# Half of the conditioning's steps in the top-16 search instead of the delta rule, and the low parts of 68 down tiles on VectorE instead of GpSimd

## The chip, the core and the metric

One core of one Trainium2 chip runs one program: two transformer blocks on 512 tokens of width 1024, in fp32. The metric is the device time of one execution in microseconds; the kernel before takes 2505.04 us, the median of three runs (2502.44 to 2505.36). Engines are called as in the profile: PE (TensorE, matmuls), DVE (VectorE), ACT (ScalarE), POOL (GpSimd), SP (SyncE, whose queue issues most DMAs).

## What is computed

The first block is a mixer (a gated delta rule on one half of the width, a pooled branch on the other), and PEER, a layer of 16,384 experts of which each token uses 16 per head. The second block is modulated by a conditioning vector. Cut to what the change touches:

```python
def second_block(x, c, ada_w, ada_b, ...):
    mod_all = einsum('bd,lde->lbe', silu(c), ada_w) + ada_b      # 1 x 6*1024: six rows
    ...
def _peer(xn, w_query, sub_keys, expert_down, expert_up):        # per block of 128 tokens
    q = (xb @ w_query).reshape(t, 8, 2, 128)
    scores = einsum("thpc,hpkc->thpk", q, sub_keys)
    s1, i1 = top_k(scores[:, :, 0], 16); s2, i2 = top_k(scores[:, :, 1], 16)
    cand = s1[..., :, None] + s2[..., None, :]                   # 16 x 16 candidates a head
    top_s, top_pos = top_k(cand, 16)
    gate = softmax(top_s)
    act = gelu(einsum("td,thkd->thk", xb, expert_down[idx]))
    return einsum("thk,thkd->td", gate * act, expert_up[idx])
```

The six rows of `mod_all` depend on `c` and `ada_w` alone. They are read by the second block, which is behind PEER.

## The kernel before

**Precision.** A product of fp32 matrices is made from three matmuls (`mm3`): each operand is split in a high part, a cast to fp32r, and a low part, the rest. `split` loads a weight tile of 128 x 1024 into a buffer with the tag `raw`, casts it on ACT (L186) and subtracts on DVE or on POOL (L187), whichever its caller hands over as `lo_engine`. `wform` makes a split and eight times three matmuls with it (L197 high by high, L198 low by high, L199 high by low). The ring of `raw` buffers has four places, and splits, the conditioning and the norms share it. High and low parts have rings of their own (`wh`, `wl`: two each).

**The stages**, in the profiled execution's time: norm, projections and the pooled branch (0 to 170 us); the delta rule (170 to 370); what is left of the conditioning, and w_out (370 to 431); the norm before PEER (431 to 463); the search for the 16 best keys and candidates (`topk`, 463 to 582); decoding of the positions into key numbers (the last part of `topk`, 582 to 672); the gates, one-hot rows of keys multiplied to a dense table (`gates`, 672 to 991); eight down tiles (to 1037); the up products (to 1790); and the second block.

**The conditioning** is the generator `ada`. It makes the six rows one after another, a segment of ten steps each: eight steps load a tile of 512 KB (SP), scale it by silu(c) on ACT (L1142) and, from the second on, add it to `ada_acc` on POOL (L1144); one step splits the sum in high (ACT, L1150) and low (POOL, L1151), sums over partitions with a matrix of ones on PE (L1155, L1156) and adds to the row on DVE (L1157); the last multiplies on POOL and reduces on DVE, or multiplies and stores. The row, the high and the low part, and one more buffer in two segments, are `raw` buffers too. In the kernel before, each round of the delta rule's loop `together` takes one step, and what is left after the loop runs at its end:

```python
                next(self.side, None)
...
        for rest in (filler, self.side):
            for _ in rest:
                pass
```

`filler` is there `pool_out`, the products of the mixer's output with w_out and their addition to x.

**The down tiles.** Of 128 tiles of `expert_down` 74 (`SPILL`) are made before the up products and stored to memory; the generator `spill` yields after each. `fill(n)` takes n of them: 0, 1, 0, 1, 0, 1, 0 and 3 after the heads of the search (`FILL_QUERY`, 6 in all), 3 before each of four token tiles of decoding (12), one after every second bank of the gates (48), and what is left, 8, afterwards. The other 54 are made among the up products. For 128 of the tokens the experts' rows are gathered one by one from POOL's queue (`sparse`, L920) and multiplied on DVE (L933); so the dense tiles have 384 columns.

**The search** runs over 16 c's (a head and a half of its query): a query (`wform` on w_query, POOL low part, read by ACT at L989) one ahead, its products with the keys, and four top-16 searches on DVE. After two c's come the head's 50 candidates (L1011) and their search.

**The gates** make, for eight tokens at a time, one-hot rows A (L1106) and E (L1107) and three products B = E x gate part (L1109) on DVE, 24 matmuls (L1114), and take one step of `sparse`.

**The order** on each engine is set by a scheduler that simulates the program with its own estimate of each instruction when the kernel is built; the order in which the code issues is its input. At run time each engine goes through its list in order.

Of the kernel before, what the change touches and what calls it, by code (L numbers as in the profile page):

```python
# [5 lines left out]
F32R = mybir.dt.float32r  # L6
# [8 lines left out]
P = 128  # L15
ST = 512
NT = 4
D = 1024
# [8 lines left out]
FILL_QUERY = [0, 1, 0, 1, 0, 1, 0, 3]  # L27
# [15 lines left out]
    [(1, 4), (1, 5)], [(1, 6)],  # L43
]
ATT_ABS = [(0,), (1,)]
FILL_DECODE = 3
FILL_GATES = 2
REST = 208
# [86 lines left out]
class Net:  # L135
# [238 lines left out]
    def mixer1(self, qk):  # L374
        nc, d = self.nc, self.d
# [23 lines left out]
        with self.sb("ap1") as self.ap:  # L399
            hT = self.norm_begin()  # L400
            with self.sb("px") as self.np:
                self.np_tag, self.np_bufs = "xhat", 6
                rest = [self.norm_tile(hT, 0, small[:, 0:8])]
# [170 lines left out]
        self.tap("gc", gc)  # L574
        self.ahead = [self.split(d["w_out"][4 + k], "u", nc.gpsimd) for k in range(4)]
        with self.sb("gd") as gd:
            self.side = self.ada(gd)
            self.delta(gd, qT, kT, vb, zs, oh, ol, beta, g, gc, egc, begc, egl, masks, self.pool_out(ph, pl, oh, ol))
        return oh, ol

# [51 lines left out]
    def delta(self, gd, qT, kT, vb, zs, oh, ol, beta, g, gc, egc, begc, egl, masks, filler):  # L632
        nc, d = self.nc, self.d
# [146 lines left out]
        def together(*gens):  # L780
            live, n = list(gens), 0
            while live:
                n += 1
                if n in FILL_DELTA:
                    next(filler, None)
                next(self.side, None)
                for gen in list(live):
                    if next(gen, self) is self:
                        live.remove(gen)
# [12 lines left out]
                yield from finish(T)  # L802

        together(scans(), lane(0), lane(1), lane(2))
        for rest in (filler, self.side):
            for _ in rest:
                pass

# [1 line left out]
    def peer(self, xT, stop=None):  # L812
        nc, d = self.nc, self.d
        nb = DT // 32
        G_d = self.t(self.dp, [nb, P, P, 32], tag="gates")
        act_d = self.t(self.dp, [SPILL, P, DT], tag="acts")
        with self.sb("pact") as pact:
# [7 lines left out]
            def spill():  # L825
                for n, j in enumerate(range(SPILL)):
                    stored[j] = n
                    nc.sync.dma_start(act_d[n], self.down(pact, j, xT, nc.gpsimd))
                    yield

            filler = spill()
# [8 lines left out]
            with self.sb("pm") as pm:  # L840
                self.sparse_pool = pm, ("su",), 6
                acc = {(T, dh): self.bank() for T in range(1, NT) for dh in range(2)}
# [9 lines left out]
                for n in range(len(tiles) + LOOK):  # L852
                    if n < len(tiles):
                        j = tiles[n]
# [116 lines left out]
    def topk(self, pi, xT, stop):  # L971
        nc, d = self.nc, self.d
# [4 lines left out]
        with self.sb("pk") as pk:  # L977
# [3 lines left out]
            I = self.t(pk, [P, NT, 16, 16], U32, tag="I")  # L981
            TV = self.t(pk, [P, NT, 8, 16], tag="TV")
            TI = self.t(pk, [P, NT, 8, 16], U32, tag="TI")
            queries = {}

            def query(c):
                pm = self.wform(d["w_query"][c], xT, nc.gpsimd)
# [4 lines left out]
            for h in range(8):  # L992
                for p in range(2):
                    c = 2 * h + p
                    if c < 15:
                        query(c + 1)
                    q = queries.pop(c)
                    pss = self.bank()
                    for T in range(NT):
                        nc.tensor.matmul(pss[:, T * P:(T + 1) * P], q[:, T * P:(T + 1) * P], sk[:, c, :],  # L1000
                                         start=True, stop=True)
                    S = self.t(pk, [P, NT, P], tag="S", bufs=2)
                    nc.scalar.activation(S, pss.rearrange("p (a b) -> p a b", a=NT), AF.Copy)
                    for T in range(NT):
                        self.top16(pk, V[:, T, c, :], I[:, T, c, :], S[:, T, :], P)

                C = self.t(pk, [P, NT, 50], tag="C", bufs=2)
                off = 0
# [114 lines left out]
                nc.sync.dma_start(G_d[tb], stg)  # L1123


    def ada(self, pool):

# [1 line left out]
        nc, d = self.nc, self.d  # L1131
        cp, sc = self.mp, self.silu_c
        raw_tile = lambda dt=F32: self.t(self.wp, [P, D], dt, tag="raw", bufs=self.raw_bufs)
        self.mod = {}
        ones = self.t(pool, [P, P], F32R, tag="ones_r")
        nc.gpsimd.tensor_copy(ones, self.ones)
        for seg, name in enumerate(("sh_m", "sc_m", "gt_m", "sh_f", "sc_f", "gt_f")):
            acc = self.t(pool, [P, D], tag="ada_acc", bufs=1)
            for k in range(KT):
                raw = raw_tile()  # L1140
                nc.sync.dma_start(raw, d["ada_w"][seg, k])
# [7 lines left out]
            hi, lo = raw_tile(F32R), raw_tile(F32R)  # L1149
# [9 lines left out]
            if gate:  # L1159
                g = raw_tile()  # L1160
                n = 1 if name == "gt_m" else 2
# [297 lines left out]
```

## Time and profile before

| | us |
|---|---|
| median of three runs | 2505.04 |
| lowest and highest run | 2502.44, 2505.36 |
| profiled execution, its own time | 2507.3 |
| its span | 2505.5 |
| busy: PE, DVE, POOL, ACT | 2286.2, 1729.1, 1056.4, 944.4 |
| mean granted clock of PE | 0.962 |

A row of a timeline gives the start, the length, the engine, the line and operation, what is written <- what is read, and in brackets how long the engine stood idle ahead of it and what ended that. Neighbouring instructions of one kind are one row with their count, and the length is then that of the run. A row of a group gives the count, the busy time, the mean of one in ns, and the idle time before the group with what ended most of it; a row by tile or line gives lowest, middle and highest duration in ns. The page's slices show PE at nine tenths or more from 1000 us on, and below before that; that earlier part is where the change lies.

### The profile page before, as it was taken

The page shows a single profiled execution, that of the slowest core. Times are in us where ns is not written, and L with a number is a line of the kernel's source. Part 1 is how long each engine was busy: PE and PEld are TensorE (multiplying, and loading weights), DVE is VectorE, ACT ScalarE, POOL GpSimd, SP SyncE. Part 2 cuts the span into 40 slices and gives each one's busy share as a digit, 9 for nine tenths or more (in the row PEclk, how much of TensorE's full clock was granted, in tenths as well). Part 3 has the DMA queues.
Part 4 walks back from the last instruction along what each step waited for, and adds up shares of the span by engine and source line. Part 5 has one row for each costly group of instructions (what it writes and reads, how often), then busy time and mean ns, then how long its engine had stood idle before and what let it go on. Part 6 is the DMA issues. An engine that isn't in the chain of part 4 may idle for free.

```text
span 2505.5 us, 31798 instructions
## 1 busy us (share of the span) xinstructions
PE 2286.2 (91%) x11953; PEld 1924.0 (77%) x11953; DVE 1729.1 (69%) x2741; ACT 944.4 (38%) x1416; POOL 1056.4 (42%) x613
## 2 busy tenths in 40 slices
PE   7978972996788889999999999999899999999998
PEld 6758751885788888888888888888777666888887
DVE  6685532799699997488787888888855664433334
ACT  4254233333333333333333333333436665422222
POOL 4356356246655555465555565665312331000000
PEclk9989985998899999999999999999999999999999
DMA  4223244322577777789899999998531121422231
GB/s 159 68 84 119 68 152 150 121 94 87 198 253 273 267 250 264 256 303 330 309 327 312 338 325 333 317 333 304 173 118 42 43 68 59 135 95 93 91 100 60
DMA packets 179851, 467.91 MB, mean 187 GB/s; under 512 B 15344, under 2 KB 83952, under 8 KB 178032
## 3 DMA queue, kind: packets, MB, share of 16 engines
q1 hardware_dynamic: 141824, 329.33, 38.8%
q0 software_dynamic: 36864, 134.23, 15.0%
q10 hardware_dynamic: 1008, 2.31, 0.3%
q8 instruction: 93, 1.52, 0.2%
q14 instruction: 62, 0.51, 0.1%
HBM read 420.86 MB, written 44.96 MB: 186 GB/s over the span
## 4 chain that ended last, share of the span: by engine, by line
PE 48%; DVE 3%; DMA 3%; issue 2%; POOL 1%; ACT 1%; SPq 0%; DVEq 0%; POOLq 0%; ACTq 0%
PE bank L198 15%; PE bank L197 15%; PE bank L199 15%; PE bank L1336 4%; DMA raw<-in_e_down_dram 1%; DMA act<-acts 1%; DVE ul L187 1%; POOL wl L187 1%; DVE su L933 0%; DVE x L939 0%; DMA raw<-in_f_out_dram 0%; ACT uh L186 0%; POOL su L920 0%; DVE act L866 0%; DMA raw<-in_e_up_dram 0%
## 5 line engine op out<-in xcount | busy, mean ns | idle before, releaser
L199 PE MATMUL bank<-actT_h,wl 128*128 128x384 f32 (+2 forms) x1672 | 596.9, 357 | 70.4 <-POOL wl L187 70.4
L197 PE MATMUL bank<-actT_h,wh 128*128 128x384 f32 (+2 forms) x1672 | 599.8, 359 | 15.2 <-ACT actT_h L328 11.6
L198 PE MATMUL bank<-actT_l,wh 128*128 128x384 f32 (+2 forms) x1672 | 591.1, 354 | 1.2 <-DVE actT_l L330 1.2
L187 POOL TENSOR_TENSOR wl<-raw,wh 128x1024 fp32r<-128x1024 f32 x157 | 416.4, 2654 | 269.6 <-ACT wh L186 175.8
L186 ACT ACTIVATE wh<-raw 128x1024 fp32r<-128x1024 f32 x190 | 201.1, 1058 | 588.4 <-issue 366.8
L199 PEld LDWEIGHTS bank<-actT_h,wl 128*128 128x128 f32 x1672 | 319.6, 191 | 107.3 <-POOL wl L187 85.6
L197 PEld LDWEIGHTS bank<-actT_h,wh 128*128 128x128 f32 x1672 | 320.3, 192 | 41.5 <-ACT actT_h L328 12.8
L198 PEld LDWEIGHTS bank<-actT_l,wh 128*128 128x128 f32 x1672 | 320.2, 192 | 24.5 <-DVE actT_l L330 1.4
L186 ACT ACTIVATE uh<-raw 128x1024 fp32r<-128x1024 f32 x194 | 202.9, 1053 | 279.6 <-PE bank L199 143.7
L187 DVE TENSOR_TENSOR ul<-raw,uh 128x1024 fp32r<-128x1024 f32 x167 | 227.1, 1363 | 117.3 <-ACT uh L186 116.7
L197 PE MATMUL bank<-uh,ah 128*128 128x512 f32 x768 | 303.8, 396 | 0.3 <-ACT ah L867 0.3
L199 PE MATMUL bank<-uh,al 128*128 128x512 f32 x768 | 302.5, 396 | 1.6 <-DVE al L868 1.6
L198 PE MATMUL bank<-ul,ah 128*128 128x512 f32 x768 | 303.8, 396 | 0.0
L920 POOL DMA_INDIRECT su<-in_e_up_dram,rows_of x128 | 195.1, 1524 | 173.2 <-DVE x L939 150.3
L259 POOL TENSOR_TENSOR rs<-ms,nhalf 128x1 f32<-128x1 f32 (+1 forms) x23 | 15.6, 679 | 446.0 <-DVE ms L258 446.0
L1109 DVE TENSOR_TENSOR B<-E,g 128x1024 bf16<-128x1024 bf16 x144 | 190.3, 1372 | 0.0
L939 DVE SCALAR_TENSOR_TENSOR x<-su,own_act,x 128x1024 f32<-128x1024 f32 x128 | 178.7, 1396 | 1.1
L199 PEld LDWEIGHTS bank<-uh,al 128*128 128x128 f32 x768 | 144.3, 188 | 37.2 <-DVE al L868 2.5
L197 PEld LDWEIGHTS bank<-uh,ah 128*128 128x128 f32 x768 | 144.3, 188 | 33.6 <-ACT ah L867 1.4
L198 PEld LDWEIGHTS bank<-ul,ah 128*128 128x128 f32 x768 | 144.3, 188 | 32.6
L920 POOL DMA_INDIRECT su<-in_e_rows_dram,rows_of x76 | 106.3, 1399 | 96.7 <-DVE su L933 81.8
L866 DVE TENSOR_TENSOR act<-act,G 128x384 f32<-128x384 f32 x128 | 91.7, 730 | 76.2 <-DMA act<-acts 45.3
(392 smaller groups left out, 3833.6 us busy)
## 6 DMA issues: line engine op xcount, KB each, us to landing
raw<-in_e_down_dram SPq DMA_DIRECT2D x128, 512.0 KB
raw<-in_e_up_dram SPq DMA_DIRECT2D x128, 512.0 KB
raw<-in_ada_w_dram SPq DMA_DIRECT2D x48, 512.0 KB
gates<-stg SPq DMA_DIRECT2D x12, 2048.0 KB
G<-gates SPq DMA_DIRECT2D x32, 768.0 KB
raw<-in_f_in_dram SPq DMA_DIRECT2D x44, 512.0 KB
acts<-act SPq DMA_DIRECT2D x74, 192.0 KB
act<-acts SPq DMA_DIRECT2D x74, 192.0 KB
```

Source lines behind the costliest of these rows:

```text
L186: nc.scalar.activation(hi, raw, AF.Copy)
L187: (lo_engine or nc.vector).tensor_sub(lo, raw, hi.bitcast(F32))
L197: nc.tensor.matmul(ps, l[0], r[0], start=start, stop=False)
L198: nc.tensor.matmul(ps, l[0], r[1], start=False, stop=False)
L199: nc.tensor.matmul(ps, l[1], r[0], start=False, stop=stop)
L259: nc.gpsimd.tensor_tensor(r, ms, self.nhalf.to_broadcast([P, n]), op=OP.pow)
L866: nc.vector.tensor_tensor(av, av, G[:, :, j % 4, :], op=OP.mult)
L920: nc.gpsimd.indirect_dma_start(out=t, out_offset=None, in_=down if n < P else up, in_offset=bass.IndirectOffsetOnAxis(ap=self.rows_of[:, n ...
L939: nc.vector.scalar_tensor_tensor(x0, t, act[:, c:c + 1], x0, op0=OP.mult, op1=OP.add)
L1109: made = nc.vector.tensor_tensor(B[:, k], E, bc(parts[k]), op=OP.mult)
L1336: self.nc.tensor.matmul(o, l, r, start=start, stop=stop, skip_group_check=True)
```

## The change

Two things. First, `ada` takes a step only in the first 30 rounds of the delta rule (`ADA_DELTA`), which are the first three of its six segments. The other 30 steps are taken in the search, two after each c; 15 of the 16 c's suffice. `ada_acc` is allocated in the search's pool there, and the matrix of ones in a pool that lives longer. Second, the low part of a down tile made ahead is subtracted on DVE if it is the seventh or a later one: 68 tiles, which are the 12 in decoding, the 48 in the gates and the 8 behind them. Those in the search and those among the up products stay on POOL.

```diff
+ADA_DELTA = 30
 ...
         with self.sb("gd") as gd:
-            self.side = self.ada(gd)
+            ada, self.ada_pool = self.ada(), gd
+            self.ada_steps = lambda n: [next(ada, None) for _ in range(n)]
 ...
                 if n in FILL_DELTA:
                     next(filler, None)
-                next(self.side, None)
+                if n <= ADA_DELTA:
+                    self.ada_steps(1)
 ...
         together(scans(), lane(0), lane(1), lane(2))
-        for rest in (filler, self.side):
-            for _ in rest:
-                pass
+        for _ in filler:
+            pass
 ...
                 for n, j in enumerate(range(SPILL)):
                     stored[j] = n
-                    nc.sync.dma_start(act_d[n], self.down(pact, j, xT, nc.gpsimd))
+                    lo = nc.gpsimd if n < sum(FILL_QUERY) else nc.vector
+                    nc.sync.dma_start(act_d[n], self.down(pact, j, xT, lo))
                     yield
 ...
-            queries = {}
+            queries, self.ada_pool = {}, pk
 ...
                     for T in range(NT):
                         self.top16(pk, V[:, T, c, :], I[:, T, c, :], S[:, T, :], P)
+                    self.ada_steps(2)
 ...
-    def ada(self, pool):
+    def ada(self):
 ...
-        ones = self.t(pool, [P, P], F32R, tag="ones_r")
+        ones = self.t(cp, [P, P], F32R, tag="ones_r")
 ...
-            acc = self.t(pool, [P, D], tag="ada_acc", bufs=1)
+            acc = self.t(self.ada_pool, [P, D], tag="ada_acc", bufs=1)
```

The lines behind the changed ones have numbers up to four higher in the changed kernel: L187 becomes L188, L933 L936, L1106 L1110, L1107 L1111, L1109 L1113, L1144 L1148, L1155 L1159.

**PE at the end of the delta rule**, before: `raw` is the high or low part of a conditioning segment, `uh` and `ul` w_out's parts, `oh` and `ol` the mixer's output; bank_2553 is the second half of token tile 1, bank_2708 tile 2.

```order
L199 MATMUL bank_2553<-uh_2403,ol_97 128x512
L1156 MATMUL bank_2538<-raw_2535,ones_r_1299 128x512
L1156 MATMUL bank_2542<-raw_2535,ones_r_1299 128x512
L1155 MATMUL bank_2608<-raw_2604,ones_r_1299 128x512
L1155 MATMUL bank_2612<-raw_2604,ones_r_1299 128x512
L1156 MATMUL bank_2608<-raw_2605,ones_r_1299 128x512
L1156 MATMUL bank_2612<-raw_2605,ones_r_1299 128x512
L1155 MATMUL bank_2658<-raw_2654,ones_r_1299 128x512
L1155 MATMUL bank_2662<-raw_2654,ones_r_1299 128x512
L197 MATMUL bank_2708<-uh_2385,oh_96 128x512
```

The same place of the change (bank_2507 is tile 1's second half, bank_2558 tile 2):

```order
L200 MATMUL bank_2507<-uh_2389,ol_97 128x512
L198 MATMUL bank_2507<-uh_2395,oh_96 128x512
L199 MATMUL bank_2507<-ul_2396,oh_96 128x512
L200 MATMUL bank_2507<-uh_2395,ol_97 128x512
L198 MATMUL bank_2558<-uh_2377,oh_96 128x512
L199 MATMUL bank_2558<-ul_2378,oh_96 128x512
L200 MATMUL bank_2558<-uh_2377,ol_97 128x512
```

The matmuls of three segments that stood between the products of tile 1 and those of tile 2 have left this place.

**POOL in the search**, before, where the low parts of queries and down tiles follow one another:

```order
L187 TENSOR_TENSOR wl_3027<-raw_3024,wh_3026 128x1024
L187 TENSOR_TENSOR wl_3125<-raw_3122,wh_3124 128x1024
L187 TENSOR_TENSOR wl_3189<-raw_3186,wh_3188 128x1024
L187 TENSOR_TENSOR wl_3287<-raw_3284,wh_3286 128x1024
L187 TENSOR_TENSOR wl_3321<-raw_3318,wh_3320 128x1024
```

The change there, around the end of a segment (L1155 is the low part of the conditioning's sum, L1173 the multiplication of its row):

```order
L1148 TENSOR_TENSOR ada_acc_2874<-ada_acc_2874,raw_3124 128x1024
L188 TENSOR_TENSOR wl_3169<-raw_3166,wh_3168 128x1024
L1148 TENSOR_TENSOR ada_acc_2874<-ada_acc_2874,raw_3128 128x1024
L188 TENSOR_TENSOR wl_3203<-raw_3200,wh_3202 128x1024
L1155 TENSOR_TENSOR raw_3267<-ada_acc_2874,raw_3266 128x1024
L188 TENSOR_TENSOR wl_3284<-raw_3281,wh_3283 128x1024
L1173 TENSOR_TENSOR raw_3264<-raw_3264,consts_68 128x1024
L1148 TENSOR_TENSOR ada_acc_3345<-ada_acc_3345,raw_3349 128x1024
L188 TENSOR_TENSOR wl_3390<-raw_3387,wh_3389 128x1024
```

Between two low parts of weights there now stand one or two instructions of the conditioning.

**DVE in the gates**, before, a little over one period (`uh` and `ul` at L933 are gathered rows):

```order
L933 SCALAR_TENSOR_TENSOR uh_5092,own_act_2925<-uh_5092,xs_2912 128x1024
L1109 TENSOR_TENSOR B_5390<-E_5389,g_981_5004 128x1024
L1109 TENSOR_TENSOR B_5390<-E_5389,g_982_5005 128x1024
L1109 TENSOR_TENSOR B_5390<-E_5389,g_983_5006 128x1024
L933 SCALAR_TENSOR_TENSOR ul_5165,own_act_2925<-ul_5165,xs_2912 128x1024
L1107 TENSOR_TENSOR E_5462<-keys_4998,i2b_5001 128x1024
L1106 TENSOR_TENSOR A_5461<-keys_4998,i1b_5000 128x1024
```

The same place of the change:

```order
L936 SCALAR_TENSOR_TENSOR ul_5165,own_act_2775<-ul_5165,xs_2762 128x1024
L188 TENSOR_TENSOR wl_5353<-raw_5350,wh_5352 128x1024
L1110 TENSOR_TENSOR A_5461<-keys_4998,i1b_5000 128x1024
L1111 TENSOR_TENSOR E_5462<-keys_4998,i2b_5001 128x1024
L1111 TENSOR_TENSOR E_5535<-keys_4998,i2b_5001 128x1024
L188 TENSOR_TENSOR wl_5426<-raw_5423,wh_5425 128x1024
L1110 TENSOR_TENSOR A_5534<-keys_4998,i1b_5000 128x1024
L1110 TENSOR_TENSOR A_5609<-keys_4998,i1b_5000 128x1024
L1113 TENSOR_TENSOR B_5463<-E_5462,g_981_5004 128x1024
L1113 TENSOR_TENSOR B_5463<-E_5462,g_982_5005 128x1024
L1113 TENSOR_TENSOR B_5463<-E_5462,g_983_5006 128x1024
L936 SCALAR_TENSOR_TENSOR uh_5238,own_act_2775<-uh_5238,xs_2762 128x1024
```

Two low parts of down tiles stand in DVE's list for every two periods, beside the one-hot rows of both, and the products B follow them.

## The prediction

> **What bounds the kernel now.** I read the engines' line and the chain that ended last first, then busy times cut into the stretches that the change touches: what the conditioning leaves after the delta rule, the search (its last 14 us apart), decoding, gates, and the eight down tiles behind the gates.
>
> ```profile
> PE 2286.2 (91%) x11953; PEld 1924.0 (77%) x11953; DVE 1729.1 (69%) x2741; ACT 944.4 (38%) x1416; POOL 1056.4 (42%) x613
> PE 48%; DVE 3%; DMA 3%; issue 2%; POOL 1%; ACT 1%; SPq 0%; DVEq 0%; POOLq 0%; ACTq 0%
> core 0: us, PE busy (x) PEld busy (x) DVE busy (x) ACT busy (x) POOL busy (x), PEclk, DMA share, GB/s
> 358.00:431.00 73.00, 18.63 (x57) 13.02 (x55) 18.41 (x18) 24.69 (x24) 52.44 (x23) 0.62 0.47 154
> 462.90:568.00 105.10, 104.34 (x541) 90.51 (x540) 96.30 (x703) 36.92 (x54) 45.04 (x19) 1.00 0.31 102
> 568.00:582.00 14.00, 14.00 (x83) 14.00 (x82) 13.96 (x103) 5.13 (x8) 6.00 (x4) 1.00 0.41 134
> 582.00:672.00 90.00, 54.39 (x287) 52.33 (x286) 68.63 (x147) 27.37 (x43) 64.88 (x21) 0.83 0.43 147
> 672.00:991.00 319.00, 283.05 (x2295) 264.10 (x2295) 314.53 (x336) 114.25 (x190) 165.30 (x91) 0.98 0.75 253
> 991.00:1037.00 46.00, 40.89 (x219) 40.25 (x218) 3.43 (x2) 14.95 (x20) 26.14 (x15) 0.93 0.89 301
> ```
>
> Over the whole, TensorE sets the time (91%), but the stages differ: in the first stretch nobody is full (PE 18.6 of 73 us), the search is full on PE (104.3 of 105.1), decoding is full on nobody, the gates are full on DVE (314.5 of 319). So four separate sums.
>
> **1. Conditioning behind the delta rule: −64.** The times are start and length of merged runs.
>
> ```profile
> 355.41 0.60 ACT L762 ACTIVATE o<-bank 128x512 f32<-128x512 f32 x1 [8.08 <-PE bank L752]
> 365.84 1.05 PE L774 MATMUL bank<-consts,o 128*128 128x128 f32 x4
> 376.66 14.45 POOL L1144 TENSOR_TENSOR ada_acc<-ada_acc,raw 128x1024 f32<-128x1024 f32 x6
> 392.25 1.22 PE L1155 MATMUL bank<-raw,ones_r 128*128 128x512 f32 x2 [21.48 <-ACT raw L1150]
> 417.45 1.22 PE L1155 MATMUL bank<-raw,ones_r 128*128 128x512 f32 x2 [21.55 <-ACT raw L1150]
> 418.47 0.63 PE L197 MATMUL bank<-uh,oh 128*128 128x512 f32 x1
> 426.25 0.40 PE L199 MATMUL bank<-uh,ol 128*128 128x512 f32 x1
> 443.24 1.04 PE L320 MATMUL bank<-consts,raw 128*128 128x128 f32 x8
> 462.60 0.58 ACT L989 ACTIVATE q<-bank 128x512 f32<-128x512 f32 x1
> ```
>
> The delta rule's last bank is read at 355.4 and its output is transposed at 365.8. Then PE stands twice for 21.5 us at L1155: the matmul of a conditioning segment waits for ACT's high part, and that for eight POOL adds (six take 14.45). Behind it in PE's queue stand the w_out products of tile 2 (418.47 to 426.65: 24 in 8.2 us, 0.43 apart cold, 0.23 at the end). Tile 3's products end at 443.24, and the first query is read 19.4 us later. The change takes 30 steps out, and no ada matmul stands before those products. From transposed output at about 363 follow 60 products (half of tile 1, tiles 2 and 3) at 0.23 to 0.34 apart, 14 to 20 us, and tile 0's transposes, 2 us: end near 379 instead of 443.24, **−64**. Bounds: PE with nothing but these 60 after 355.4 gives 367 (−76); all cold and waiting for x-norms of ACT, 385 (−58).
>
> **2. The search: +30.** It gets the 30 steps, two after each of 15 c's: 21 adds, 3 low parts and 3 multiplications on POOL, 24 scales and 3 high parts on ACT, 6 adds and 2 reduces on DVE, 12 matmuls, 29 more transfers on SP's queue.
>
> ```profile
> L187 POOL TENSOR_TENSOR wl<-raw,wh 128x1024 fp32r<-128x1024 f32 x22 | 52.8, 2402 | 72.5 <-ACT wh L186 72.5
> L1144 POOL TENSOR_TENSOR ada_acc<-ada_acc,raw x42: 2337/2354/2826, 180.8 to 414.0; 128x1024 f32<-128x1024 f32 x42
> 377.89 1.15 ACT L1142 ACTIVATE raw<-raw,silu_c 128x1024 f32<-128x1024 f32 x1 [1.49 <-DMA raw<-in_ada_w_dram]
> 395.51 1.28 DVE L1157 TENSOR_TENSOR raw<-raw,bank 128x512 f32<-128x512 f32 x2 [17.56 <-PE bank L1156]
> 399.25 1.22 DVE L1170 TENSOR_REDUCE sc_f<-raw 128x8 f32<-128x1024 f32 x1 [2.46 <-POOL raw L1169]
> L1011 DVE TENSOR_TENSOR C<-V x64: 141/166/2232, 470.0 to 582.3; 128x8 f32<-128x8 f32 x24, 128x32 f32<-128x32 f32 x8, 128x20 f32<-128x20 f32 x8, 128x16 f32<-128x16 f32 x8
> ```
>
> POOL gains 27 × 2.354 = 63.6 beside 45 + 6 = 51 us in 119: 115, as long as PE's span. ACT goes from 42 to 42 + 27 × 1.15 = 73, DVE from 110 by about 8 to 118, PE by 3. Each engine alone fits. DVE is the nearest to full; if its waits of now stay as they are, its added 8 us are the lower bound: +8. Above it come queues. Splits, queries and conditioning share four raw buffers, and at a segment's end row, high and low part hold three of them until the reduce. That chain is low part 2.4, matmuls and adds 1.28 + 1, POOL's multiplication 2.35 (the reduce waited 2.46), reduce 1.22, and behind it a fresh query's scale 1.15 and low part 2.4: about 12 us, of which PE has 2 to 4 of products in hand, so 9 idle, three times: 27. Three more for DVE adds that meet a POOL instruction (L1011: 166 ns in the middle, 2232 at worst): **+30**. Upper bound: every moved POOL instruction stops the chain for its whole length, +64. I take the middle since two of three steps go in while PE has a query's products ahead.
>
> **3. Decoding: −18.**
>
> ```profile
> L199 PE MATMUL bank<-actT_h,wl 128*128 128x384 f32 x93 | 33.5, 360 | 30.9 <-POOL wl L187 30.9
> 601.64 30.32 POOL L187 TENSOR_TENSOR wl<-raw,wh 128x1024 fp32r<-128x1024 f32 x2 [2.42 <-ACT wh L186]
> 629.67 0.69 PE L199 MATMUL bank<-actT_h,wl 128*128 128x384 f32 x1 [24.58 <-POOL wl L187]
> 641.93 5.88 DVE L1047 TENSOR_TENSOR oh<-pa,io 128x2048 bf16<-128x2048 bf16 x1
> 647.74 1.21 DVE L1047 TENSOR_TENSOR oh<-pb,io 128x2048 bf16<-128x2048 bf16 x1
> ```
>
> Two POOL splits beside running DVE take 30.3 us instead of 4.8, and PE waits 24.6 for them; the other way round L1047 takes 5.88 instead of 1.21. The Trainium skill has the rule ("SBUF — State Buffer", section "Who interferes with whom"): a DVE instruction with two SBUF inputs contends with a GpSimd one that reads SBUF, and the loser blocks for the whole instruction. Both rows agree.
>
> With 12 splits on DVE the contention goes. DVE's 68.6 busy holds some 16 of it (L1047 alone 4.7 an instance), leaving 53; 12 splits at 1.22 add 15: 68, and a few waits for PE and transposes: 72 of 90, **−18**. Bounds: the 30.9 less the added splits' own queueing behind DVE, −26; if DVE's order puts a split late and PE waits again, −5.
>
> **4. Gates: −40.** One period of 48 (start, length):
>
> ```profile
> 827.50 1.21 DVE L933 SCALAR_TENSOR_TENSOR uh<-uh,xs 128x1024 f32<-128x1024 f32 x1
> 828.64 0.68 DVE L1107 TENSOR_TENSOR E<-keys,i2b 128x1024 bf16<-128x1024 bf16 x1
> 829.25 0.68 DVE L1106 TENSOR_TENSOR A<-keys,i1b 128x1024 bf16<-128x1024 bf16 x1
> 829.85 4.48 DVE L1109 TENSOR_TENSOR B<-E,g 128x1024 bf16<-128x1024 bf16 x3
> 834.25 1.22 DVE L933 SCALAR_TENSOR_TENSOR ul<-ul,xs 128x1024 f32<-128x1024 f32 x1
> 830.18 2.39 POOL L187 TENSOR_TENSOR wl<-raw,wh 128x1024 fp32r<-128x1024 f32 x1
> 829.80 1.56 PE L1114 MATMUL bank<-B,A 128*128 128x128 bf16 x24
> 836.56 1.56 PE L1114 MATMUL bank<-B,A 128*128 128x128 bf16 x24
> L199 PE MATMUL bank<-actT_h,wl 128*128 128x384 f32 x381 | 133.7, 351 | 34.5 <-POOL wl L187 34.5
> L187 DVE TENSOR_TENSOR wl<-raw,wh x47: 1215/1224/2985, 427.8 to 2466.2; 128x1024 fp32r<-128x1024 f32 x47
> ```
>
> DVE's period is 834.25 − 827.50 = 6.75. Three B's take 4.40 though E and A, as large, start 0.61 apart: 3 × 0.61 = 1.83. The excess of 2.57 is the one POOL split of 2.39 that lies inside. Clean, DVE needs 1.14 + 0.61 + 0.60 + 1.83 = 4.18, and with its own split (1.224, about 1.15 start to start) 5.33. PE needs per period what it has without its waits: 283 / 48 = 5.9 by the window, whose matmul ends are modelled long; 6.76 from gate group to gate group less some 0.9 of waiting (34.5 / 48 = 0.72 for POOL's splits alone) gives 5.8. So PE becomes the bound at 5.8: 48 × 5.8 = 279 against 319, **−40**. Bounds: DVE at 5.33 with PE's overlap, 5.5 × 48 = 265 (−54); DVE's queue making PE wait a quarter of a period, 6.1 × 48 = 294 (−25). The transfers of a period (319 us at 253 GB/s over 48: 1.7 MB) would go at 290 GB/s, while the down tiles after the gates run at 301.
>
> **5. The rest: −3.** Eight tiles after the gates have DVE free (3.4 of 46 us) and PE at 40.9: −4, bounds 0 and −5. The cast of `ones` now stands early in POOL's order, ahead of the first weights' low parts: +1 (0 to 2). The first 30 steps lie in the delta rule as before, and nothing there is added.
>
> **Sum**: −64 + 30 − 18 − 40 − 4 + 1 = −95 from the profiled execution's own 2507.3: 2412. That execution lies 2.3 above the median of the runs (2505.04), so **2410**.
>
> **Rivals.**
> A, *the search hides the steps*. For it: every engine's sum fits under 119 us, and DMA there is at 0.31. Against: four raw buffers, three of them held at a segment's end. The search then costs DVE's +8 alone: 2388.
>
> B, *the search goes at POOL's pace*. The queue of POOL is in order: a query's low part waits behind adds, and an add behind a transfer; with 115 us of work in 119 any gap is lost, and every one of 27 instructions prolongs it by 2.354: +64, 2444. Against: the steps come two at a time between queries whose splits run one ahead.
>
> C, *DVE stays the bound of gates and decoding*. If the low parts come late in DVE's order, or the B's stay slow beside the gathers that POOL still issues, gates and decoding give 5 each: +35 + 13, 2458. Against: the excess of 2.57 matches the POOL split of 2.39 and no gather's length.
>
> D, *the other side: the raw ring turns serial*. Queries, fills and steps take some 55 raw buffers in the search (16 queries, 6 fills, 33 or 34 for the steps). If a transfer is issued only when the buffer's last reader is through and nothing overlaps, each costs a landing (1.49 waited at 377.89, 3 or more from issue), scale 1.15 and POOL 2.35. The search now has 119; it eats up the gain of all other terms (125) when it passes 244, or 4.4 us a buffer. At 5.2 it is 286, +167 in place of +30: 2547. Against: in the stretch 358 to 431 the six adds of 14.45 run one behind another, 2.4 apart, so the ring does deliver there.
>
> That the change does not do what it says is excluded by the order of the instructions: the adds stand in the search and the splits on DVE.
>
> **How the numbers follow.** The forecast, 2392 to 2428 as its own range: 55%. A and still better, 20%; B, 15%; C, 7%; D, 3%. The range 2372 to 2447 takes in A and most of B; what is left out is C, D and the far end of A, some 15%. What can be told from no change is 0.2%, 5 us: faster by more 0.96, within 0.01, slower 0.03 (D).
>
> **What would show it.** Step 1: no PE wait of 21 us at the conditioning's matmuls, the first query read near 399. Step 2: the search about 149 us long, with three PE gaps of 8 to 10 us at segment ends; even gaps at every c speak for B, none for A. Step 3: no POOL instruction above 3 us in decoding, L1047 near 1.2 throughout. Step 4: three B's in 1.9 us, a period of 5.8 with PE without gaps; if DVE is still back to back, C. The forecast is wrong if the search grows by over 60, or if a gate period stays above 6.4.

## The result, and the profile after

The changed kernel takes **2396.53 us**, the median of four runs (2390.32 to 2398.71), against 2504.16 before: a ratio of **0.9567, interval 0.9547 to 0.9587**. The forecast was 2410, its own range 2392 to 2428, the whole range 2372 to 2447. The profiled execution took 2390.32 (span 2388.5), which is 6 below the median; its stretches below add up to 117 us saved, the medians to 108.

The engines' line and the chain that ended last, of the changed kernel:

```profile
PE 2270.4 (95%) x11953; PEld 1919.0 (80%) x11953; DVE 1686.1 (71%) x2809; ACT 950.6 (40%) x1416; POOL 884.9 (37%) x545
PE 77%; DVE 9%; issue 4%; DMA 3%; ACT 3%; POOL 3%; DVEq 0%; SPq 0%; POOLq 0%; ACTq 0%
```

PE went from 91% to 95% of a shorter span with as many matmuls; POOL lost 68 instructions and 172 us. To cut both executions at the same places I took the first or last instruction of a line. Of the changed kernel these are, with lowest, middle and highest duration in ns and first and last start in us:

```profile
L764 ACT ACTIVATE o<-bank x4: 597/598/600, 259.9 to 354.2; 128x512 f32<-128x512 f32 x4
L992 ACT ACTIVATE q<-bank x16: 577/579/598, 393.4 to 519.8; 128x512 f32<-128x512 f32 x16
L1015 DVE TENSOR_TENSOR C<-V x64: 140/161/2432, 402.0 to 538.6; 128x8 f32<-128x8 f32 x24, 128x32 f32<-128x32 f32 x8, 128x20 f32<-128x20 f32 x8, 128x16 f32<-128x16 f32 x8
L1113 DVE TENSOR_TENSOR B<-E,g x144: 675/682/692, 612.3 to 869.5; 128x1024 bf16<-128x1024 bf16 x144
L1118 PE MATMUL bank<-B,A x1152: 217/218/312, 613.0 to 880.8; 128*128 128x128 bf16 x192
L198 PE MATMUL bank<-uh,ah x768: 390/396/504, 931.0 to 1690.6; 128*128 128x512 f32 x192
```

Of the kernel before, the two that the prediction did not show:

```profile
L1114 PE MATMUL bank<-B,A x1152: 217/218/308, 673.5 to 988.4; 128*128 128x128 bf16 x192
L197 PE MATMUL bank<-uh,ah x768: 390/396/628, 1043.2 to 1806.9; 128*128 128x512 f32 x192
```

| stretch (us) | before | after | moved | forecast |
|---|---|---|---|---|
| start to the delta rule's last output (L764) | 355.4 | 354.2 | −1.2 | +1 |
| to the first query read (L992) | 107.2 | 39.2 | −68.0 | −64 |
| search, to the last candidate sum (L1015) | 119.7 | 145.2 | +25.5 | +30 |
| decoding, to the first B (L1113) | 90.4 | 73.7 | −16.7 | −18 |
| gates, to the last gate matmul (L1118) | 315.7 | 268.5 | −47.2 | −40 |
| to the first up product | 54.8 | 50.2 | −4.6 | −4 |
| up products | 763.7 | 759.6 | −4.1 | 0 |
| rest | 698.6 | 697.9 | −0.7 | 0 |
| sum | 2505.5 | 2388.5 | −117.0 | −95 |

The busy times in the stretches that moved (changed kernel):

```profile
core 0: us, PE busy (x) PEld busy (x) DVE busy (x) ACT busy (x) POOL busy (x), PEclk, DMA share, GB/s
354.00:393.40 39.40, 34.16 (x208) 29.52 (x207) 21.94 (x38) 20.13 (x38) 3.69 (x6) 1.00 0.25 83
393.40:538.60 145.20, 124.12 (x588) 104.37 (x589) 137.11 (x816) 69.33 (x84) 110.10 (x47) 0.93 0.54 182
538.60:612.30 73.70, 61.87 (x331) 60.35 (x330) 67.74 (x160) 29.91 (x47) 27.09 (x9) 0.93 0.56 195
612.30:880.80 268.50, 267.76 (x2280) 259.54 (x2280) 252.27 (x381) 118.99 (x188) 56.39 (x44) 0.99 0.85 299
880.80:931.00 50.20, 48.35 (x270) 47.70 (x268) 17.70 (x12) 18.41 (x27) 14.15 (x9) 0.97 0.87 309
```

The bound has changed hands twice. In the gates DVE was full and PE was not; now PE is busy 267.8 of 268.5 us. In the search PE was full; now DVE is busy 137.1 of 145.2 and PE 124. DVE's busy time there grew from about 110 to 137, and only 8 us of that is work that moved there. The groups of DVE that tell why, in a window that ends just behind the last sums; before:

```profile
L1011 DVE TENSOR_TENSOR C<-V 128x8 f32<-128x8 f32 (+2 forms) x64 | 15.4, 290 | 0.0
L1014 DVE TENSOR_TENSOR C<-V 128x32 f32<-128x32 f32 x8 | 2.1, 261 | 0.0
```

and of the changed kernel:

```profile
L1015 DVE TENSOR_TENSOR C<-V 128x8 f32<-128x8 f32 (+2 forms) x64 | 31.1, 528 | 0.0
L1018 DVE TENSOR_TENSOR C<-V 128x32 f32<-128x32 f32 x8 | 5.1, 634 | 0.0
```

The 72 sums of candidates take 36.2 us instead of 17.5. Their work is the same, and half of those at L1015 still take 0.16 us; the longest takes 2.43, which is the length of one POOL instruction of 128 x 1024 (2.40). On the timelines of the changed kernel such a sum ends together with a POOL instruction, here at 410.98 and 410.93:

```profile
408.73 2.25 DVE L1018 TENSOR_TENSOR C<-V 128x32 f32<-128x32 f32 x1
408.56 2.37 POOL L188 TENSOR_TENSOR wl<-raw,wh 128x1024 fp32r<-128x1024 f32 x1 [0.65 <-ACT wh L187]
```

And the three PE gaps of 8 to 10 us at segment ends, which were to show the prediction's reason, aren't there. PE's waits in the changed kernel's search are short and many (us in total, times, longest):

```profile
PE bank L198 <- ACT wh L187: 7.9, 7, 3.5
PE bank L200 <- POOL wl L188: 6.7, 4, 2.8
PE bank L1003 <- ACT q L992: 4.5, 4, 1.3
PE bank L1159 <- ACT raw L1154: 2.3, 1, 2.3
```

That is not what the prediction said of the search, so most experiments are on it.

### The profile page after: what moved, and what is told of

The parts are those of the page before. It is cut to its first block, busy times and chain, and to the rows that moved or that the text cites. A ratio compares the mean times of both kernels' runs of the same rounds, so it can differ in the third digit from the quotient of the medians.

```text
span 2388.5 us, 31780 instructions
## 1 busy us (share of the span) xinstructions
PE 2270.4 (95%) x11953; PEld 1919.0 (80%) x11953; DVE 1686.1 (71%) x2809; ACT 950.6 (40%) x1416; POOL 884.9 (37%) x545
## 3 DMA queue, kind: packets, MB, share of 16 engines
q1 hardware_dynamic: 141824, 329.33, 40.7%
## 4 chain that ended last, share of the span: by engine, by line
PE 77%; DVE 9%; issue 4%; DMA 3%; ACT 3%; POOL 3%; DVEq 0%; SPq 0%; POOLq 0%; ACTq 0%
PE bank L198 22%; PE bank L200 22%; PE bank L199 22%; PE bank L1340 4%; PE bank L1118 3%; PE bank L645 2%; DVE x L942 1%; DMA raw<-in_e_down_dram 1%; DVE cy L470 1%; DMA raw<-in_ada_w_dram 1%; POOL wl L188 1%; DVE cy L468 1%; ACT uh L187 1%; DVE ul L188 1%; POOL ada_acc L1148 1%
## 5 line engine op out<-in xcount | busy, mean ns | idle before, releaser
L200 PE MATMUL bank<-actT_h,wl 128*128 128x384 f32 (+2 forms) x1672 | 589.1, 355 | 12.0 <-POOL wl L188 8.3
L187 ACT ACTIVATE wh<-raw 128x1024 fp32r<-128x1024 f32 x190 | 201.0, 1059 | 421.1 <-PE bank L199 267.4
L198 PEld LDWEIGHTS bank<-actT_h,wh 128*128 128x128 f32 x1672 | 319.2, 191 | 49.4 <-ACT actT_h L329 12.8
L187 ACT ACTIVATE uh<-raw 128x1024 fp32r<-128x1024 f32 x194 | 203.0, 1053 | 290.1 <-PE bank L200 146.5
L188 POOL TENSOR_TENSOR wl<-raw,wh 128x1024 fp32r<-128x1024 f32 x89 | 225.0, 2529 | 175.5 <-ACT wh L187 81.2
L188 DVE TENSOR_TENSOR ul<-raw,uh 128x1024 fp32r<-128x1024 f32 x167 | 225.8, 1356 | 74.8 <-ACT uh L187 74.0
L188 DVE TENSOR_TENSOR wl<-raw,wh 128x1024 fp32r<-128x1024 f32 x115 | 140.4, 1222 | 114.2 <-ACT wh L187 112.9
```

The source lines that it names most:

```text
L187: nc.scalar.activation(hi, raw, AF.Copy)
L188: (lo_engine or nc.vector).tensor_sub(lo, raw, hi.bitcast(F32))
L198: nc.tensor.matmul(ps, l[0], r[0], start=start, stop=False)
L200: nc.tensor.matmul(ps, l[1], r[0], start=False, stop=stop)
```

## The experiments

The times in the experiments are medians, and the stretches are cut as above. Theory one is the prediction's: the ring of four raw buffers stalls PE at each segment's end. Theory two is contention: DVE's sums of two operands wait for POOL's instructions, and DVE is full.

### The two halves alone

The first half alone leaves all low parts on POOL; the second half alone is the kernel before with the line of `spill`.

```diff
 # e1_ada_only: the changed kernel with
-                    lo = nc.gpsimd if n < sum(FILL_QUERY) else nc.vector
+                    lo = nc.gpsimd
 # e2_lo_only: the kernel before with
-                    nc.sync.dma_start(act_d[n], self.down(pact, j, xT, nc.gpsimd))
+                    lo = nc.gpsimd if n < sum(FILL_QUERY) else nc.vector
+                    nc.sync.dma_start(act_d[n], self.down(pact, j, xT, lo))
```

> Only the first half of the change: the 30 conditioning steps in the search, every low part of a down tile on POOL as before. From the changed kernel's trace, stage by stage against the kernel before: behind the delta rule -69, search +25, and decoding (90.4) and gates (315.7) as before. So about 2504 - 44 = 2460. If the two halves need one another (for instance since POOL is busy longer), decoding or gates differ from before by more than 5 us.

> Only the second half: low parts of 68 down tiles on DVE, the conditioning as before. Decoding -17, gates -47, the eight tiles behind them -5, the rest as before: about 2504 - 69 = 2435; a gate period of 5.6 us with PE full. If the halves are additive, the two losses of this and of the other half add to the whole change's 108.

The first half: 2485.01 us (2474.36 to 2494.40), ratio 0.9919 (0.9896 to 0.9942). The second: 2431.17, ratio 0.9712 (0.9695 to 0.9728). By stretch:

| | behind the delta rule | search | decoding | gates | up to the first up product | rest |
|---|---|---|---|---|---|---|
| before | 107.2 | 119.7 | 90.4 | 315.7 | 54.8 | 698.6 |
| first half | 39.1 | 150.5 | 104.5 | 315.8 | 54.6 | 705.5 |
| second half | 104.5 | 120.2 | 69.6 | 268.1 | 50.8 | 697.1 |
| both | 39.2 | 145.2 | 73.7 | 268.5 | 50.2 | 697.9 |

The second half is 4 us better than expected, and each of its stretches is within 4 us of where it was forecast. The first half is 25 us worse than expected: decoding took 104.5 instead of 90.4, the second block 7 more, and the search 6 more than its forecast. In decoding POOL's low parts still meet DVE's two-operand instructions. Groups of POOL and PE in decoding of the first half alone:

```profile
L188 POOL TENSOR_TENSOR wl<-raw,wh 128x1024 fp32r<-128x1024 f32 x15 | 62.9, 4199 | 35.6 <-ACT wh L187 35.6
L200 PE MATMUL bank<-actT_h,wl 128*128 128x384 f32 x109 | 39.6, 365 | 33.0 <-POOL wl L188 33.0
```

Of the fifteen splits half take 2.40 us or less and one takes 25.08, which makes the mean 4.2. PE waits 33 us for them, as it waited 31 before; the wait itself did not grow. What grew is PE's work: decoding holds 51 more instructions of PE than before (336 against 285, 65.2 us of work against 54.1), which are products of down tiles that the longer search had not got done: its PE did 583 instructions where the kernel before did 626, though 12 of the 583 are the conditioning's. So 11 of these 14 us belong to the search. The changed kernel has 331 there, and hides them, since PE no longer waits for POOL. The second block's 7 us go with the scheduler's order: POOL's list of instructions there is the changed kernel's in the kernel before, in the second half and in the fastest kernel below, but another one in this kernel and in three others below. These four took 705 to 708 us there, where the others (but for two with more work in that block) took 696 to 699. That the order is the cause was not tested by itself. The gains of the halves, 19 and 73, add to 92 of the 108; what is missing is in these two places.

### The candidate sums with an operand in PSUM

ACT copies the 16 best values of the first half of the query to a bank of PSUM, and the sums on DVE read them there. So a sum has one operand in SBUF instead of two.

```diff
                 C = self.t(pk, [P, NT, 50], tag="C", bufs=2)
+                vb = self.bank()[:, 0:NT * 16].rearrange("p (a b) -> p a b", a=NT)
+                nc.scalar.activation(vb, V[:, :, 2 * h, :], AF.Copy)
 ...
-                                            V[:, :, 2 * h, a:a + 1].to_broadcast([P, NT, nb]), op=OP.add)
+                                            vb[:, :, a:a + 1].to_broadcast([P, NT, nb]), op=OP.add)
 ...
-                nc.vector.tensor_tensor(C[:, :, 42:50], V[:, :, 2 * h, 8:16],
+                nc.vector.tensor_tensor(C[:, :, 42:50], vb[:, :, 8:16],
```

> The changed kernel, with one operand of the head's candidate sums copied by ACT to PSUM, so that DVE's sums read one operand from SBUF and one from PSUM. Theory of the raw ring (the prediction's: PE stands at the three segment ends for 27 us): the search stays at 145 us, give or take 3. Theory of contention (DVE is full, its two-input sums wait for POOL's instructions, 35 us for them instead of 16): each sum falls from 0.51 us in the mean to about 0.15, DVE's busy time by some 24, and the search goes from 145 to 122 to 130 us.

2382.65 us (2377.28 to 2387.40), 14 less than the changed kernel; the search 134.8 instead of 145.2. Groups of DVE in its search:

```profile
L1017 DVE TENSOR_TENSOR C<-V,bank 128x64 f32<-128x64 f32 (+3 forms) x64 | 6.2, 185 | 0.0
L1020 DVE TENSOR_TENSOR C<-bank,V 128x32 f32<-128x32 f32 x8 | 1.6, 200 | 0.0
L967 DVE MAX8 V<-S 128x8 f32<-128x128 f32 x64 | 14.5, 282 | 22.6 <-ACT S L1006 22.4
```

The sums take 7.8 us instead of 36.2, and none is held up (the longest takes 0.23): the contention is shown, and it hangs on the second operand in SBUF. But the search fell by 10 only, where theory two forecast 122 to 130 us for it. DVE now stands idle for 22.6 us, waiting for scores; something else was next in line.

### Raw buffers of their own for the steps

```diff
-        raw_tile = lambda dt=F32: self.t(self.wp, [P, D], dt, tag="raw", bufs=self.raw_bufs)
+        def raw_tile(dt=F32):
+            if seg < 3:
+                return self.t(self.wp, [P, D], dt, tag="raw", bufs=self.raw_bufs)
+            return self.t(self.ada_pool, [P, D], dt, tag="ada_raw", bufs=4)
```

> The changed kernel, with four raw buffers of their own for the 30 conditioning steps in the search, so that queries and down tiles no longer wait for a buffer that a segment holds. Theory of the raw ring: the search falls from 145 us by 15 to 27. Theory of contention: it stays at 140 to 145, and the sums keep their mean of 0.5 us.

2397.42 us, 1 more than the changed kernel, and a search of 154.2. Theory one, as the only cause, falls. The sums (DVE, search of this kernel):

```profile
L1015 DVE TENSOR_TENSOR C<-V 128x8 f32<-128x8 f32 (+2 forms) x64 | 40.9, 688 | 0.0
```

They did not stay at 0.53 us in the mean and the search not at 140 to 145, as theory two had it; they rose to 0.69. With its second line (7.3) the sums take 48.2 us here, and what is left of the search is 106.0. The executions compared below under the changed kernel again leave about the same rest, 106 to 109.

### Both edits together

This kernel has the two diffs above.

> The changed kernel with both edits to the search, the sums' operand in PSUM and four raw buffers of their own for the steps. Alone they took 10 us and gave 9. What keeps the search at 135 us with the operand in PSUM: if it is the raw ring, which was hidden behind DVE, the search falls to 120 to 126; if it is POOL's queue (109 us of work in order, low parts of queries behind adds), it stays at 133 to 140.

**2366.43 us** (2364.23 to 2370.76), ratio 0.9449 (0.9430 to 0.9467): the fastest of all. The search takes 123.8 us, 4 more than before the change, with 30 conditioning steps in it. Its busy times, in a window that ends behind the last sums:

```profile
393.70:519.00 125.30, 118.39 (x607) 102.59 (x607) 111.39 (x820) 62.57 (x86) 101.64 (x43) 0.99 0.54 183
```

PE is busy 118 of 125 us again. (The last run below, whose code of the search is the same, took 126.1.) So both theories hold, one behind the other. While DVE waits for POOL, more raw buffers win nothing; once it does not, they win the 11 us from 134.8 to 123.8. Alone the edits gave 14 us and nothing by the medians, together 30.

### The changed kernel again

The kernel is the changed one, unaltered; there is no diff.

> The changed kernel once more, unaltered, beside the two others. Two kernels whose search has the same instructions in the same order gave 150.5 and 156.0 us for it where the first execution gave 145.2, and the sums' group took 38.9 and 40.9 us instead of 29.7. If contention makes the difference, this search lies between 144 and 157, and its length less the sums' group is 111 to 116 once more.

2395.67 us (2388.55 to 2402.10). The search took 155.3 us. With the first half alone and with the run on the gates below there are four executions of one and the same list of instructions in the search. Their sums, 64 of them (the changed kernel's row stands above), in the order first half, gates, again:

```profile
L1015 DVE TENSOR_TENSOR C<-V 128x8 f32<-128x8 f32 (+2 forms) x64 | 38.9, 654 | 0.0
L1015 DVE TENSOR_TENSOR C<-V 128x8 f32<-128x8 f32 (+2 forms) x64 | 42.2, 700 | 0.0
L1015 DVE TENSOR_TENSOR C<-V 128x8 f32<-128x8 f32 (+2 forms) x64 | 46.6, 770 | 0.0
```

With the eight of the other line (5.1, 5.4, 7.2, 2.6) all sums take 36.2, 44.3, 49.4 and 49.2 us, and the searches 145.2, 150.5, 156.0 and 155.3: without the sums 109.0, 106.2, 106.6 and 106.1. The expectation took the sums of the one line, from windows that ended before the last few, and gave 111 to 116 for the difference; so counted it was 110. With all sums counted, the search's length follows the contention to within 3 us. The runs of the changed kernel lie 8 to 14 us apart, as much as these searches do; those of the kernel before lay 3 apart at first and 7 to 11 in later sets, so not all of it need come from here. The profiled execution of the result was a lucky one: the search costs 25 to 36 us.

### The steps in the attention instead

```diff
-                    self.ada_steps(2)                       # in the search
 ...
             for n in range(len(units) + 2):                 # in attention
 ...
+                self.ada_steps(2)
                 if n >= len(units) - 3 - LEAD0:
```

(`ada_pool` is attention's own there.)

> The changed kernel, with its 30 later conditioning steps not in the search but in the attention of the second block, two after each of its first units, where POOL was busy 20 to 38% and DMA moved 44 to 58 GB/s. The search should be what it was before the change, 120 us instead of 145, whatever made it longer. If the attention hides the steps (PE is 98% busy there, so only 12 matmuls of 0.4 us add to it), the rest after the up products stays at 698 to 703, and the whole is 2396 - 25 + 3 = 2374. If POOL's adds hold DVE up there as in the search, the rest grows by 15 or more and the whole stays above 2386.

2409.94 us, 13 more than the changed kernel. The search is back at 119.7, as expected, but the rest grew by 46. The stretch of attention from its first exponential to its last, of the changed kernel and then of this one:

```profile
1780.00:1978.80 198.80, 196.83 (x864) 130.99 (x863) 125.64 (x174) 126.65 (x229) 64.86 (x46) 1.00 0.18 56
```

```profile
1753.00:1997.40 244.40, 229.32 (x904) 146.96 (x904) 157.27 (x187) 148.62 (x257) 123.12 (x66) 0.93 0.28 93
```

POOL is busy 58 us longer, DVE 32, PE's clock falls to 0.93 with its gaps, and the attention pays 46. POOL at 33% and DVE at 63% had room there, but PE was busy 197 of 199 us, so whatever holds PE up lengthens the stage. The contention is there again. Two groups of DVE, of the changed kernel and then of this one (windows from the last up product to behind the attention):

```profile
L1356 DVE TENSOR_TENSOR L1l<-x,L1h 128x768 fp32r<-128x768 f32 x8 | 8.6, 1079 | 0.0
L1388 DVE SCALAR_TENSOR_TENSOR x<-bank,e 128x384 f32<-128x384 f32 (+1 forms) x32 | 19.5, 621 | 12.5 <-ACT e L1387 10.2 <-POOL x L1403 1.7 <-POOL L1h L1355 0.4
```

```profile
L1357 DVE TENSOR_TENSOR L1l<-x,L1h 128x768 fp32r<-128x768 f32 x8 | 12.7, 1585 | 0.1
L1389 DVE SCALAR_TENSOR_TENSOR x<-bank,e 128x384 f32<-128x384 f32 (+1 forms) x32 | 19.1, 620 | 11.5 <-ACT e L1388 6.1 <-POOL x L1404 5.1
```

The group with both operands in SBUF takes 1.59 us each instead of 1.08; the one with an operand in a bank of PSUM stays at 0.62. How much of the 46 us is contention, and how much the raw ring, was not taken apart.

With the sums' operand in PSUM as well (the two diffs together):

> The same, with the candidate sums' operand in PSUM as well. With the steps out of the search only some 20 low parts on POOL are left to hold up the sums: 16 us of them before the change, of which 6 would stay. PE was full in the search then, so the gain is that in the last 14 us, where DVE alone works: 0 to 5 us of the search's 120. If DVE sets the whole search it is 8 to 10.

2398.98 us; the search 116.9 instead of 119.7. So contention costs a search without the steps 3 us, within the 0 to 5 expected where PE sets the pace.

### DVE's share in the gates

```diff
-                    for k in range(3):
+                    for k in range(2):
                         made = nc.vector.tensor_tensor(B[:, k], E, bc(parts[k]), op=OP.mult)
 ...
-                                                 B[:, k, 2 * j + t // 2, :, t % 2],
+                                                 B[:, min(k, 1), 2 * j + t // 2, :, t % 2],
```

> The changed kernel, with the third of the three gate products B on DVE left out; PE's matmuls read the second one twice, so PE has as much to do, and the gates lose their lowest digits. DVE has 0.61 us less in each of 48 periods. If PE sets the gates' pace in the changed kernel, they stay at 266 to 269 us; if DVE does, they fall to 240 to 245.

The gates took 267.8 us instead of 268.5, as expected if PE sets the pace. Their busy times:

```profile
621.50:889.30 267.80, 267.06 (x2280) 259.51 (x2280) 224.91 (x334) 113.61 (x189) 52.27 (x44) 0.99 0.84 300
```

DVE's busy time fell by 27 and nothing came of it. (The whole took 2402.17: the search was a long one of 156.0, and the second block in the other order took 708.0.)

### The last segments without their matmuls

The kernel before, in which PE has nothing to do for the last three segments:

```diff
-            for dh in range(2):
+            for dh in range(2 if seg < 3 else 0):
                 ps = self.bank()
```

> The kernel before, with the matmuls on PE and the additions on DVE of the last three conditioning segments left out (their rows lack the weighted sum); all of their transfers, scales and POOL's adds stay where they were. The prediction's reason for the 107 us behind the delta rule is PE's queue: w_out's products stand behind the segments' matmuls. By it the first query is read some 40 to 50 us after the delta rule, as in the changed kernel (39). Rival: POOL's queue. The norm's reciprocal roots stand on POOL behind all of the conditioning's adds, whose last starts near 414. By it the norm can't begin before about 420, and the part stays at 90 us or more, though w_out's products are done by 380.

The stretch behind the delta rule took 101.5 us instead of 107.2, where the prediction's reason gave 40 to 50. (The whole, in one execution, 2509.71; the second block in the other order.) Rows of POOL, ACT, DVE and PE, from its timelines by engine:

```profile
376.01 0.69 DVE L630 TENSOR_TENSOR x<-x,bank 128x512 f32<-128x512 f32 x1 [2.11 <-PE bank L199]
399.93 16.88 POOL L1144 TENSOR_TENSOR ada_acc<-ada_acc,raw 128x1024 f32<-128x1024 f32 x7 [2.36 <-ACT raw L1142]
411.60 1.15 ACT L1142 ACTIVATE raw<-raw,silu_c 128x1024 f32<-128x1024 f32 x1 [1.30 <-DMA raw<-in_ada_w_dram]
423.85 1.06 ACT L186 ACTIVATE wh<-raw 128x1024 fp32r<-128x1024 f32 x1 [5.95 <-DMA raw<-in_w_query_dram]
424.81 1.04 ACT L276 ACTIVATE raw<-x 128x1024 f32<-128x1024 f32 x1
426.31 0.56 POOL L259 TENSOR_TENSOR rs<-ms,nhalf 128x1 f32<-128x1 f32 x1 [3.33 <-DVE ms L258]
429.02 1.97 PE L320 MATMUL bank<-consts,raw 128*128 128x128 f32 x8 [53.05 <-ACT raw L308]
```

Free of the conditioning, PE has w_out's products of tiles 1 and 2 done by 376, and then stands for 53 us: the norm of the tokens is in ACT's list behind the conditioning's scales and behind a query weight's cast (423.85), which waits for its transfer, and on POOL behind its adds. ACT scales the last conditioning tile at 411.60, at the pace of load, scale and add, 2.3 to 2.9 us a tile. So PE's queue cost 6 us, or 3: in the second half alone, which has the kernel before's instructions there, the stretch took 104.5. The rest was the same hold on ACT's, POOL's and the raw ring's order. The raw ring came last in this run: the query weight's transfer is issued at 420.34, just when POOL's last low part (done at 420.32) has freed a buffer, and ACT's cast waits 5.95 us for it. POOL came close behind: it ends its last step at 422.98 and then stands idle 3.33 us ahead of the norm's first root (426.31), so without that wait the norm could have come some 3 us earlier at most.

### 40 steps in the delta rule, and four tiles a time in decoding

Both start from the fastest kernel. The first has `ADA_DELTA = 40` (and buffers of their own from the fifth segment on), the second `FILL_DECODE = 4`.

> The kernel with both edits to the search (own raw buffers for the steps, the sums' operand in PSUM), and 40 instead of 30 steps in the delta rule, so that two segments are left for the search. POOL has 9 instructions less in the search (22 us of 102), which then should be PE's: 118 to 121 us instead of 124. The fourth segment's matmuls come back before the end of the delta rule; in the kernel before they cost PE 6 us at 365, so the part behind the delta rule goes from 40 to 42 to 46. Together no gain that can be told, or 3 us either way, around 2366.

2373.11 us, 7 more than the fastest, where 3 either way was expected. The search fell to 118.5, but the stretch behind the delta rule rose from 40.7 to 47.4, past the 42 to 46 expected; a fourth segment costs there more than it gives in the search.

> The kernel with both edits to the search (own raw buffers for the steps, the sums' operand in PSUM; 2366), and four instead of three down tiles ahead of each token tile of decoding, so that four are left behind the gates instead of eight. PE was busy 61 of 71 us in decoding, DVE 67. If PE's gaps there can be filled, decoding grows by 4 x 4.4 - 10 = 8 us and the part behind the gates falls by 4 x 4.4 = 18: 2356. If DVE, with four more low parts at 1.22, sets decoding, its waits stay, decoding grows by the whole 18 and nothing is won: 2366.

2378.80 us, 12 more, where 10 less or no change was expected. Decoding grew from 71.4 to 81.9, nearer the 8 us of a PE that is filled up than the 18 of a full DVE, but the part behind the gates fell from 49.0 to 41.3 only, not by 18: PE is busy for 32 of the 41 us there and waits for casts of weights, with DMA at 309 GB/s. That the transfers set it is likely and was not tried. The other 10 us are the second block, which the scheduler put in its other order (707.3 instead of 696.8).

## Why the prediction was right or wrong

**Step 1, the conditioning behind the delta rule: size right (−64 against −68.0), reason wrong.** "Behind it in PE's queue stand the w_out products" is true in the trace, and was worth 3 to 6 us. The two waits of 21.5 us on PE were seen since PE had products to do; without these matmuls it waits as long at the norm (53.05), because ACT and POOL have the norm behind the same steps. The estimate survived since the change takes the steps out of all queues at once. That the size came out is luck in part: I read the wait of one engine and did not ask what the next instruction would wait for. (The lower bound of 367 should be 369: 60 products at 0.23 us take 13.8.)

**Step 2, the search: size within its spread (+30 against +25.5, and +31 to +36 in three other executions), mis-split.** The prediction gave the raw ring at segment ends 27 us and DVE's meetings with POOL 3. Measured, DVE's meetings came first: its sums rose by 18.7 to 31.9 us, and the ring counted only once they were gone, with 11. That 27 + 3 came near the measured sum is luck. The row it had quoted, 166 ns in the middle and 2232 at worst, showed it: 17.5 us of sums before, for work that takes 7.6 without contention, so each of 22 POOL instructions already cost DVE 0.45 us on average, and there were to be 27 more. The Trainium skill ("SBUF — State Buffer", section "Who interferes with whom") says that a DVE instruction with at most one SBUF input, outside the modes in which DVE uses two ports, does not contend with GpSimd; the runs with the operand in PSUM agree (0.165 us in the mean). Rival B was right that every moved POOL instruction has a price, which measured 0.9 to 1.3 us (25.5 to 36.3 by 27) and not 2.354, and it was DVE that paid. A fell, and D too.

**Step 3, decoding: right (−18 against −16.7).** No POOL split is left beside the bf16 instructions; L1051 takes 1.22 us in all eight (group of the changed kernel):

```profile
L1051 DVE TENSOR_TENSOR oh<-pa,io 128x2048 bf16<-128x2048 bf16 x4 | 4.9, 1216 | 0.0
L1051 DVE TENSOR_TENSOR oh<-pb,io 128x2048 bf16<-128x2048 bf16 x4 | 4.9, 1218 | 0.0
```

DVE's busy time less its 14 splits (17.1) is 50.6, near the 53 of the forecast.

**Step 4, gates: right in kind, mis-sized by 7 (−40 against −47.2).** PE became the bound; the waits for POOL's splits are gone and three B's take 1.89 us (the highest single one 692 ns, where it was 5607). The term that was off is PE's period: 5.8 forecast, 268.5 / 48 = 5.59 measured. The one period that it was taken from, 6.76, was longer than the mean, 315.7 / 48 = 6.58, and the other source, 5.9, is a busy time that holds modelled ends of matmuls. Rival C fell.

**Step 5:** −4.6 for −4, and no cost of the early cast that could be seen (−1.2). The up products' −4.1 were not forecast, and no run shows their cause.

The sum, −95, was 22 short of the −117 between the two profiled executions: 7 in step 4, 4 or 5 each in step 1, in step 2 and in the up products, and 2 ahead of the delta rule's end. Of the medians' −108 it was 13 short, since the changed kernel's profiled execution lies 6 below its median and that of the kernel before 3 above. The sizes were worked out from rows and held; the reasons of steps 1 and 2 did not.

## What to carry to other kernels

Before work moves to an engine that looks idle, look at its neighbour: here GpSimd had room, but its long instructions stopped short two-operand sums on a full VectorE, at 0.6 to 0.9 us of VectorE's time for each of the 47, and moving one of their operands to PSUM was worth 14 of the 25 to 36 us that the move had cost. When several queues are held by the same work, a wait on one of them names only the first hold; leave that one out and see what waits next. Where two bounds stand one behind the other, judge the edits together: alone they gave 14 us and nothing, both gave 30.

## What the runs showed of the hardware

- The same instructions in the same order took 145 to 156 us in four executions, and the difference is the time of 72 short DVE sums, 36 to 49 us. Whether a sum of 0.16 us meets a POOL instruction of 2.4 is settled anew in each execution, so a stage that is full on VectorE becomes 11 us wide.
- With the second operand read from PSUM the 64 sums of the one line took 0.165 us in the mean beside 102 us of POOL work in 125.
- A stage with POOL at 33%, DVE at 63% and PE at 99% grew by 46 us when it got 30 steps, while the search of before, with POOL at 43%, DVE at 92% and PE at 99%, grew by 25 to 36, and by 4 once contention and buffers were dealt with (in the attention that was not tried). The busy shares of POOL and DVE did not tell which would grow less.
